# A two-layer trunk in fp32: compression by strided operands, full-width splits with moves by DMA, mixer outputs in the stream's tile

## The chip, the core and the metric

One of the eight cores of a Trainium2 chip runs the kernel. Its engines are TensorE (PE: matmuls and transposes; PEld is the loading of its stationary operand), VectorE (DVE), ScalarE (ACT), GpSimd (POOL) and SyncE (SP), which here issues the DMA transfers. Every engine runs its own instructions strictly in the order in which they stand. The metric is the device time of one execution in microseconds (us).

## What is computed

Two layers over 512 tokens of 1024 channels, all in float32. A layer projects the stream once, gives the columns to three token mixers, joins their outputs by one projection, normalises, and runs a feed-forward block:

```python
def reference(x, w_in, cmp_pos, cmp_w1, ...):
    for l in range(DEPTH):
        proj = h @ w_in[l]
        nq, nkv, ngate, gq, gk, gv, glr, gog, pu = jnp.split(proj, split_points, axis=-1)
        mixed = jnp.concatenate([nsa_mixer(nq, nkv, ngate, ...),     # 6 query heads, 2 kv heads
                                 gla_mixer(gq, gk, gv, glr, gog, ..., gla_norm_g[l]),
                                 pool_mixer(pu, pool_w[l], pool_scale[l])], axis=-1)
        h = layer_norm(DEEPNORM_ALPHA * h + mixed @ w_out[l], ...)
        ff = jnp.square(jax.nn.relu(h @ w_up[l])) @ w_down[l]
        h = layer_norm(DEEPNORM_ALPHA * h + ff, ...)

# in nsa_mixer: 31 blocks of 32 tokens, 16 apart, are compressed to one key and one value each
    def compress(t, p, w1, w2):
        tb = t[:, :, blk_idx] + p                 # blk_idx = 16 n + 0..31; p: position table
        hid = jax.nn.gelu(tb.reshape(B, G, n_cmp, CMP_BLOCK * Dh) @ w1)
        return hid @ w2
# its three branches (compressed, selected, window) are softmax attentions with one gate per head and branch;
# pool_mixer subtracts a token from trailing means over 2, 4, 8 and 16 tokens and maps each group
```

## The kernel before

A Python program writes the instructions out. Its `Planner` (line 33) keeps a planned time for every engine and buffer; each helper (`MM`, `TR`, `act`, `tt`, `ts`, `stt`, `recip`, `dma`) emits one instruction and adds its estimated cost. Pieces of work are generators with a priority: whenever the planned TensorE time `now` has reached what a piece waits for, its next step is emitted; when none is ready, the backbone `everything()` emits more matmuls of the projections. So the estimates set the order of instructions on every engine, and the chip then runs that order. Since all calls go through helpers, all matmuls have line 177, transposes 182, ACT work 190, tensor-tensor 202, tensor-scalar 208, `stt` 215, reductions 219, reciprocals 227, loads 318. `tt(..., "any")` lets the planner choose between DVE and POOL.

Every fp32 product is three TensorE passes over fp32r halves: an operand is split by ACT into a rounded high part (`wh`, `hTh`) and by DVE or POOL into the rest (`wl`, `hTl`). Weights come by DMA as `wr` into four raw buffers and are split into four pairs of `wh`/`wl`; `splits()` does it in the order of use.

The backbone of a layer runs the blocks of `ORDER = 'ABDEFWGCOPNR'`: A, B, E, D, F, G, C, O project the stream (A and O token-major, O being the gate `og` of the linear-attention mixer in 128x384 matmuls; G the queries; D the compressed branch's keys and values and one more key; F the third key; C the pooling mixer's input; E values and gates), W is the compression, P and R the two halves of the early output projection, N its remaining rows for the first tokens; the feed-forward block follows. Attention, linear attention and pooling run as pieces beside it.

What the change touches: `im2col` builds, from the keys and values of `k0_out`/`v0_out`, tiles of 4 x 124 shifted columns plus positions (64 partitions at a time, with a step of 16 tokens), splits them, and `compress` reads them as 32 contiguous pairs of matmuls of 248 and 124 columns per program; `hidden` adds the halves. `q_out` and `k_out` split 64 partitions at a time, so that a tile holds the high half in one set of 64 partitions and the low half in the other. `u_out` makes prefix sums for windows 2 to 16: a POOL copy of the first 1, 2, 4 or 8 columns and one addition each, then a 512-column matmul with `wbd`. `head` makes scores, reduces their maxima, exponentiates on ACT (the sum goes to `den`), clamps `den`, takes the reciprocal f, multiplies it by the head's gate, scales the exponentials `s` by it on whichever engine the planner thinks first, and transposes them (`ident`). `og_out` makes the swish gate and multiplies by `ngh`, half the norm's weights broadcast to 128 partitions. `gla_mix` and the end of `head` put split mixer outputs into slots (a common pool of `NSLOT` 128x512 tiles), which `mix_parts` hands to `out_part` and `out_rest`. `new_hT` makes the tiles hTh and hTl of the transposed stream.

## Time and profile before

| | |
|---|---|
| median of 3 runs | 1217.43 us (1216.94 to 1217.57) |
| the profiled execution | 1217.37 us |
| its span, first to last instruction | 1215.6 us |
| mean granted TensorE clock | 0.994 of full |
| TensorE busy | 98% |
| DVE, ACT, POOL busy | 75%, 49%, 25% |
| DMA, mean rate | 94 GB/s |

The span is cut into instructions of five engines. A busy TensorE is not TensorE at its peak: matmuls overlap, so the distance between the starts of two is what one costs. Idle time of another engine costs nothing by itself. What ended TensorE's idle time is named behind `<-`. Layer 0 takes roughly the first 600 us and the mixers' stage the first 200 us of each layer.

### The profile page before, as it was taken

What the parts mean: (1) busy time and instruction counts of PE and PEld (TensorE: products, weight loads), DVE (VectorE), ACT (ScalarE), POOL (GpSimd) and SP (SyncE); (2) the same over time, 40 slices, a digit from 0 to 9 for tenths busy, and PEclk for the clock granted to TensorE, in tenths of its full rate; (3) what the DMA queues carried; (4) which work ended last, traced back from release to release, by engine and by line L of the source; (5) the groups of instructions that cost most, each with busy time, mean ns of one, the idle gap of its engine ahead of it and who ended that gap; (6) DMA issues with size and microseconds to landing.
All of it is one profiled execution on the core that took longest, in us unless ns stands there. A gap on an engine that the chain in (4) does not pass through costs nothing.

```text
span 1215.6 us, 19049 instructions
## 1 busy us (share of the span) xinstructions
PE 1192.5 (98%) x7305; PEld 1050.1 (86%) x7305; DVE 909.3 (75%) x1563; ACT 593.2 (49%) x1119; POOL 308.5 (25%) x332
## 2 busy tenths in 40 slices
PE   9999999999999999999999998999999999999997
PEld 7898788889889899899888977888998998998985
DVE  3699998886687476485667999979947864855846
ACT  4633666554337246255146445766633562552730
POOL 0255431234330010020132634303434200201202
PEclk9999999999999999999999999999999999999999
DMA  6514103143323333335144040121623233342331
GB/s 215 149 40 118 44 19 103 30 138 121 88 71 121 103 88 121 87 87 153 41 134 115 27 131 18 55 77 36 183 71 94 87 122 87 88 125 82 98 112 69
DMA packets 128523, 113.92 MB, mean 94 GB/s; under 512 B 17168, under 2 KB 103728, under 8 KB 128432
## 3 DMA queue, kind: packets, MB, share of 16 engines
q1 hardware_dynamic: 128432, 112.71, 31.1%
q8 instruction: 57, 0.93, 0.3%
q14 instruction: 34, 0.28, 0.1%
HBM read 110.59 MB, written 2.10 MB: 93 GB/s over the span
## 4 chain that ended last, share of the span: by engine, by line
PE 84%; DVE 11%; POOL 2%; ACT 1%; issue 1%; DMA 1%; POOLq 0%; SPq 0%; DVEq 0%
PE b L177 81%; DVE s L202 4%; PE b L182 3%; DVE s L215 2%; DVE nb L219 1%; POOL r L202 1%; DVE wl L202 1%; ACT s L190 1%; POOL s L202 1%; DVE h L215 0%; DMA h<-in_x_dram 0%; DVE s L208 0%; DMA wr<-in_w_up_dram 0%; DVE den L208 0%; DVE f L227 0%
## 5 line engine op out<-in xcount | busy, mean ns | idle before, releaser
L177 PE MATMUL b<-wh,s 128*128 128x512 f32 x1280 | 413.9, 397 | 0.5 <-ACT s L190 0.5
L202 DVE TENSOR_TENSOR wl<-wr,wh 128x1024 fp32r<-128x1024 f32 (+4 forms) x185 | 226.6, 1228 | 163.1 <-ACT wh L190 155.0
L190 ACT ACTIVATE wh<-wr 128x1024 fp32r<-128x1024 f32 (+4 forms) x194 | 184.4, 954 | 252.2 <-PE b L177 205.3
L177 PEld LDWEIGHTS b<-wh,s 128*128 128x128 f32 x1280 | 240.5, 188 | 54.9 <-ACT s L190 0.9
L177 PE MATMUL b<-wl,s 128*128 128x512 f32 x640 | 252.4, 394 | 0.0
L190 ACT ACTIVATE s<-s 128x512 fp32r<-128x512 f32 (+5 forms) x328 | 186.9, 587 | 99.1 <-DVE s L202 79.3
L177 PE MATMUL b<-s,s 128*128 128x256 f32 (+5 forms) x1296 | 183.7, 293 | 0.2
L190 ACT ACTIVATE s<-b 128x384 fp32r<-128x384 f32 (+8 forms) x230 | 106.5, 475 | 156.2 <-PE b L177 116.8
L177 PE MATMUL b<-hTh,wh 128*128 128x256 f32 (+1 forms) x544 | 176.0, 324 | 0.0
L177 PE MATMUL b<-hTh,wl 128*128 128x256 f32 (+1 forms) x544 | 174.6, 321 | 0.0
L177 PE MATMUL b<-hTl,wh 128*128 128x256 f32 (+1 forms) x544 | 174.4, 321 | 0.0
L177 PEld LDWEIGHTS b<-s,s 128*128 128x128 f32 (+1 forms) x1296 | 163.2, 190 | 5.2 <-DVE s L202 1.4
L202 DVE TENSOR_TENSOR s<-s,s 128x512 fp32r<-128x512 f32 (+6 forms) x190 | 145.2, 774 | 21.6 <-ACT s L190 16.0
L202 DVE TENSOR_TENSOR s<-b,s 128x256 f32<-128x256 f32 (+7 forms) x262 | 123.9, 482 | 46.4 <-PE b L177 38.1
L177 PEld LDWEIGHTS b<-wl,s 128*128 128x128 f32 x640 | 120.4, 188 | 26.5 <-POOL wl L202 0.7
L202 POOL TENSOR_TENSOR s<-wr 128x512 f32<-128x512 f32 x24 | 39.1, 1631 | 319.8 <-DMA wr<-in_w_up_dram 288.3
L177 PEld LDWEIGHTS b<-hTh,wl 128*128 128x128 f32 x544 | 102.5, 188 | 8.6
L177 PE MATMUL b<-hTh,s 128*128 128x256 f32 x576 | 109.9, 284 | 0.0
L177 PEld LDWEIGHTS b<-hTh,wh 128*128 128x128 f32 x544 | 102.5, 189 | 8.2
L177 PEld LDWEIGHTS b<-hTl,wh 128*128 128x128 f32 x544 | 102.5, 188 | 8.0
L202 POOL TENSOR_TENSOR s<-s,s 128x512 f32<-128x512 f32 (+5 forms) x54 | 72.7, 1348 | 135.7 <-DVE s L202 73.5
L177 PEld LDWEIGHTS b<-hTh,s 128*128 128x128 f32 x576 | 92.1, 191 | 0.1
(150 smaller groups left out, 1618.4 us busy)
## 6 DMA issues: line engine op xcount, KB each, us to landing
wr<-in_w_down_dram SPq DMA_DIRECT2D x64, 512.0 KB, 3.8
wr<-in_w_up_dram SPq DMA_DIRECT2D x52, 512.0 KB, 4.0
wr<-in_w_out_dram SPq DMA_DIRECT2D x20, 512.0 KB, 3.5
wr<-in_w_in_dram SPq DMA_DIRECT2D x24, 384.0 KB, 3.2
...
wr<-in_w_in_dram SPq DMA_DIRECT2D x6, 512.0 KB, 3.7
h<-in_x_dram SPq DMA_DIRECT2D x4, 512.0 KB, 8.4
```

The costliest lines, as they stand in the source:

```text
L177: nc.tensor.matmul(o, a, b, start=start, stop=stop, **({"skip_group_check": True} if loose else {}))
L182: nc.tensor.transpose(o, a, i)
L190: nc.scalar.activation(o, a, func, scale=scale, **kw)
L202: e.tensor_tensor(out=o, in0=a, in1=b, op=op)
L215: nc.vector.scalar_tensor_tensor(o, a, s, b, op0=op0, op1=op1)
L219: nc.vector.tensor_reduce(o, a, axis=AX.X, op=op, negate=negate)
```

## The change

- Compression: `im2col` is gone. Keys and values are split into a tile X of 128 x 8 x 560 (`to_windows`); two DMAs of `move`, SBUF to SBUF on SP's queue, put the copy shifted by one token into the other 64 partitions. `positions` writes the position table into 32 further columns, as another block. `compress` reads X with a step of 16 elements, 2 x 2 x 2 x 34 = 272 columns and 136 for the low pass; `hidden` takes the positions' contribution from one column (`hb`) and adds it.
- A move is a plain `dma_start` with both sides bitcast to fp32; the planner counts 0.5 us on the queue and 2.0 to the landing.
- Queries and keys: one full-width ACT instruction and one DVE or POOL instruction per tile instead of halves, and three or six moves of 64x512.
- `u_out`: the copies of the first columns go from POOL to ACT.
- `head`: f is made by one DVE instruction, min with 1e30 and product with the gate, instead of clamp on DVE and product on POOL or DVE.
- `og_out`: no product with `ngh`; the w_out rows are scaled instead when they are split (`scaled`, with `gsc` of 128x3).
- Mixer outputs go into the slices of hT that the stream no longer needs, behind the event `gone` of block O; compressed probabilities and two of the feed-forward's token sums go into tiles with X's tag; `NSLOT` 46 becomes 38.
- The planner's estimate for an fp32r matmul is max(0.109, 0.006 + 0.4414e-3 n), 0.224 for fp32, 0.04 for bf16.

```diff
     def MM(o, a, b, start, stop, loose=False):
         n = b.free_size()
-        pl.pe(max(0.025, n / 2400.0 * (4 if b.dtype == F32 else 1) + 0.0025))
+        pl.pe(max(0.109, 0.006 + 0.4414e-3 * n) if b.dtype == F32R else 0.224 if b.dtype == F32 else 0.04)
         nc.tensor.matmul(o, a, b, start=start, stop=stop, **({"skip_group_check": True} if loose else {}))
...
-            yield from split_to(hi, lo, raws[i], firsts.get(i, -0.2))
+            if i in scaled:
+                l, ks = scaled[i]
+                yield [(l, "params"), free_act]
+                for j, k in enumerate(ks):
+                    if 3 <= k < 6:
+                        act(hi[:, j], raws[i][:, j], scale=gsc[l][:, k - 3:k - 2])
+                    else:
+                        act(hi[:, j], raws[i][:, j])
+                yield
+                for j, k in enumerate(ks):
+                    yield [free_dve]
+                    if 3 <= k < 6:
+                        stt(lo[:, j], raws[i][:, j], gsc[l][:, k - 3:k - 2], hi[:, j], OP.mult, OP.subtract)
+                    else:
+                        tt(lo[:, j], raws[i][:, j], hi[:, j], OP.subtract)
+            else:
+                yield from split_to(hi, lo, raws[i], firsts.get(i, -0.2))
...
-        ngh = layer.tile([128, 384], F32, tag="ngh", name=f"ngh{l}")
+        gsc[l] = layer.tile([128, 3], F32, tag="gsc", name=f"gsc{l}")
...
             free()
-            yield
-            tt(gd, gd, ngh, OP.mult, "any")
             yield [E("on", t)]
             tt(on[t], on[t], gd, OP.mult, "any")
...
-            mh, ml = slot(n=384, dt=F32R), slot(n=384, dt=F32R)
-            act(mh, p[:, 0:384])
-            yield
-            tt(ml, p[:, 0:384], mh, OP.subtract)
+            pv = p[:, 0:384].rearrange("p (k n) -> p k n", k=3)
+            mh, ml = [a[:, 0:3, 128 * t:128 * t + 128] for a in hT]
+            act(mh, pv)
+            yield
+            tt(ml, pv, mh, OP.subtract)
             free()
-            gmix[t] = (mh, ml)
...
-            if k < 3:
-                mt, c0 = nmix[t // 2][k], 128 * (t % 2)
-                return mt[:, c0:c0 + 128], mt[:, 256 + c0:384 + c0]
             if k < 6:
-                return [a[:, 128 * (k - 3):128 * (k - 3) + 128] for a in gmix[t]]
+                return [a[:, (k + 3) % 6, 128 * t:128 * t + 128] for a in hT]
             return [a[:, 128 * t:128 * t + 128] for a in mix[k]]
...
-                    ts(nw[r, 0:sh], prev[r, 0:sh], 1.0, None, OP.mult, eng="pool")
+                    act(nw[r, 0:sh], prev[r, 0:sh])
                     tt(nw[r, sh:512], prev[r, sh:512], prev[r, 0:512 - sh], OP.add, "any")
...
+        def own(X, kv, g, part):
+            return X[64 * g:64 * g + 64, 4 * part + 2 * kv + g, 1 - g:513 - g]
+        def other(X, kv, g):
+            return [X[64 * q:64 * q + 64, 2 * kv + g:8:4, 1 - q:513 - q] for q in (1 - g, g)]
+        def to_windows(kv, src, eng):
+            X = xs[0]
+            for g in range(2):
+                act(own(X, kv, g, 0), src[64 * g:64 * g + 64])
+            yield
+            for g in range(2):
+                tt(own(X, kv, g, 1), src[64 * g:64 * g + 64], own(X, kv, g, 0), OP.subtract, eng)
+            yield
+            for g in range(2):
+                move(*other(X, kv, g))
+            yield
...
         def k0_out(ps):
-            kv0[0] = yield from rope(ps)
-            ev("k0")
+            r = yield from rope(ps)
+            yield
+            yield from to_windows(0, r, "any")
+            drop()
+            ev("im", 0)
         def v0_out(ps):
-            kv0[1] = slot()
-            act(kv0[1], ps)
+            yield from to_windows(1, ps, "dve")
             free()
-            ev("v0")
-            yield
+            ev("im", 1)
         def k_out(br):
             def out_(ps):
                 r = yield from rope(ps)
                 yield
-                res = []
-                for g in range(2):
-                    kh, kl = slot(dt=F32R), slot(dt=F32R)
-                    src = r[64 * g:64 * g + 64]
-                    act(kh[0:64], src)
-                    act(kh[64:128], src)
-                    res.append((kh, kl))
-                    yield
-                    hs = kh[64 * g:64 * g + 64]
-                    tt(kl[0:64], src, hs, OP.subtract, "any")
-                    tt(kl[64:128], src, hs, OP.subtract, "any")
+                own_ = [slot(dt=F32R), slot(dt=F32R)]
+                act(own_[0], r)
+                yield
+                tt(own_[1], r, own_[0], OP.subtract, "any")
                 drop()
-                KK[br] = res
+                yield
+                both = [slot(dt=F32R), slot(dt=F32R)]
+                for a, b in zip(both, own_):
+                    move(a[0:64], b[64:128])
+                    move(a[64:128], b[64:128])
+                yield
+                for a in own_:
+                    move(a[64:128], a[0:64])
+                yield
+                KK[br] = [own_, both]
                 ev("K", br)
             return out_
...
             def out_(ps):
                 r = yield from rope(ps)
                 yield
-                for e in range(2):
-                    q_ = slot(dt=F32R)
-                    me, ot = slice(64 * e, 64 * e + 64), slice(64 - 64 * e, 128 - 64 * e)
-                    act(q_[me], r[me], scale=0.125)
-                    yield
-                    stt(q_[ot], r[me], 0.125, q_[me], OP.mult, OP.subtract)
-                    QS[2 * m + e] = q_
-                    ev("Q", 2 * m + e)
+                q0, lo = slot(dt=F32R), slot(dt=F32R)
+                act(q0, r, scale=0.125)
+                yield
+                stt(lo, r, 0.125, q0, OP.mult, OP.subtract)
                 drop()
+                yield
+                q1 = slot(dt=F32R)
+                move(q1[0:64], q0[64:128])
+                move(q1[64:128], lo[64:128])
+                yield
+                move(q0[64:128], lo[0:64])
+                yield
+                drop()
+                QS[2 * m], QS[2 * m + 1] = q0, q1
+                ev("Q", 2 * m)
+                ev("Q", 2 * m + 1)
             return out_
-        ims = [None] * 4
-        def im2col():
...
-                            sap = bass.AP(tensor=a.tensor, offset=a.offset + t0, ap=[a.ap[0], [2, 4], [16, 31]])
...
-                            tt(imv[64 * par:64 * par + 64, :, c0:c0 + 31], sap, pa[:, :, None].to_broadcast([64, 4, 31]),
-                               OP.add, "any")
...
-                ev("im", jc)
-            drop(2)
+        xs = [big.tile([128, 8, 560], F32R, tag="X", name=f"X{l}")]
+        def positions():
...
+                act(hi, pv)
+                yield
+                tt(lo, pv, hi, OP.subtract)
+            yield
+            ev("im", 2)
         def compress():
             yield [("bank", 1)]
             ph = bank()
-            for jc in range(4):
-                yield [E("im", jc), ("split", u["W"][jc // 2])]
-                wh, wl = parts[u["W"][jc // 2]]
-                for j in range(4):
-                    kk = 4 * (jc % 2) + j
-                    hl = ims[jc][j // 2][:, j % 2]
-                    MM(ph[:, 0:248], wh[:, kk, :], hl, jc == 0 and j == 0, False, True)
-                    MM(ph[:, 0:124], wl[:, kk, :], hl[:, 0], False, jc == 3 and j == 3, True)
...
+            X = xs[0]
+            yield [E("im", i) for i in range(3)]
+            for j in range(16):
+                ui = u["W"][j // 8]
+                yield [("split", ui)]
+                wh, wl = parts[ui]
+                c0 = 1 + 2 * j
+                MM(ph[:, 0:272], wh[:, j % 8, :], X[:, :, c0:c0 + 529:16], j == 0, False, True)
+                MM(ph[:, 0:136], wl[:, j % 8, :], X[:, 0:4, c0:c0 + 529:16], False, j == 15, True)
+                if j % 8 == 7:
+                    used(ui)
...
+            hb = small(1, "hb", bufs=2)
+            hxv = hx.rearrange("p (g n) -> p g n", g=2)
+            phv = ph[:, 0:272].rearrange("p (a k g n) -> p a k g n", a=2, k=2, g=2)
+            for kv in range(2):
+                r = slice(64 * kv, 64 * kv + 64)
+                vcopy(hxv[r], phv[r, 1, kv, :, 0:31])
+                vcopy(hb[r], phv[r, 1, kv, 0, 32:33])
+                tt(hb[r], phv[r, 0, kv, 0, 32:33], hb[r], OP.add)
+                stt(hxv[r], phv[r, 0, kv, :, 0:31], hb[r], hxv[r], OP.add, OP.add)
...
-            res = slot(dt=F32R), slot(dt=F32R)
+            res = room(2 * H), room(2 * H + 1)
...
-            ts(den, den, 1e-30, None, OP.max)
             recip(f, den)
-            yield
-            tt(f, f, gate[:, 2 * H:2 * H + 2, 3 * hh + br], OP.mult, "any")
+            stt(f, f, 1e30, gate[:, 2 * H:2 * H + 2, 3 * hh + br], OP.min, OP.mult)
...
-                mt = slot(dt=F32R)
-                act(mt[:, 0:256], f_)
-                yield
-                tt(mt[:, 256:512], f_, mt[:, 0:256], OP.subtract)
+                yield [E("gone", 2 * H), E("gone", 2 * H + 1)]
+                mh, ml = [a[:, 3 + m, 256 * H:256 * H + 256] for a in hT]
+                act(mh, f_)
+                yield
+                tt(ml, f_, mh, OP.subtract)
                 drop()
-                nmix[H][m] = mt
                 ev("nmix", H, m)
...
+                if name == "O":
+                    ev("gone", t)
...
-NSLOT = 46
+NSLOT = 38
```

How the order of instructions changes at three places of layer 0. The first is TensorE's order around the pool mixer's first matmul (`wbd`). In the rows of before, `b_1443` is a 128-token tile of block O, whose weight split `wl_1451` is read there, and s_1387 and s_1421 are scaled exponentials; in the rows of after, `s_855`, `s_856` are a key's high and low parts, `s_1258` is a query and `b_1370` the first head's scores. Before:

```order
L177 MATMUL b_1443<-wh_1308,hTh_117 128x384
L177 MATMUL b_1443<-wl_1309,hTh_117 128x384
L177 MATMUL b_1443<-wh_1308,hTl_118 128x384
L177 MATMUL b_1535<-s_1452,wbd_128 128x512
L182 MATMUL b_1548<-ident,s_1387 128x128 x3
L182 MATMUL b_1556<-ident,s_1421 128x128 x3
L177 MATMUL b_1443<-wh_1450,hTh_117 128x384
L177 MATMUL b_1443<-wl_1451,hTh_117 128x384
L177 MATMUL b_1443<-wh_1450,hTl_118 128x384
```

After:

```order
L177 MATMUL b_1322<-wl_1274,hTh 128x384
L177 MATMUL b_1322<-wh_1273,hTl 128x384
L177 MATMUL b_1370<-s_855,s_1258 128x128
L177 MATMUL b_1370<-s_856,s_1258 128x128
L177 LDWEIGHTS identb
L177 MATMUL b_1370<-mdiag,identb 128x128
L177 MATMUL b_1370<-s_855,s_1258 128x256
L177 MATMUL b_1370<-s_856,s_1258 128x256
L177 LDWEIGHTS identb
L177 MATMUL b_1370<-mdiag,identb 128x128
L177 MATMUL b_1377<-s_1340,wbd_128 128x512
```

The six transposes of exponentials have left the place behind the pool mixer's matmul; a head's scores stand ahead of it now.

The second is POOL's order in the same stretch: before, the last of the prefix sums (`s_1478` to `s_1487`), the products f with the gate, the scaling of a head's exponentials, and a weight split of block O:

```order
L202 TENSOR_TENSOR s_1478<-s_1441 128x511
L208 TENSOR_SCALAR s_1481<-s_1478 128x2
L202 TENSOR_TENSOR s_1481<-s_1478 128x510
L208 TENSOR_SCALAR s_1484<-s_1481 128x4
L208 TENSOR_SCALAR s_1487<-s_1484 64x8
L202 TENSOR_TENSOR f_1327<-f_1327,gate_131 128x2
L202 TENSOR_TENSOR f_1338<-f_1338,gate_131 128x2
L202 TENSOR_TENSOR s_1421<-s_1421,f_1338 128x128
L202 TENSOR_TENSOR s_1421<-s_1421,f_1338 128x256
L202 TENSOR_TENSOR wl_1451<-wr_1224,wh_1450 128x768
```

After, from the first prefix addition of C's output to the linear mixer's products behind the split of the same unit of block O:

```order
L202 TENSOR_TENSOR s_1317<-s_1314 64x510
L202 TENSOR_TENSOR s_1348<-s_1320 128x511
L202 TENSOR_TENSOR s_1354<-s_1351 128x508
L202 TENSOR_TENSOR wl_1330<-wr_1185,wh_1329 128x768
L202 TENSOR_TENSOR s_1450<-s_1450,f_1369 128x256
L202 TENSOR_TENSOR s_798<-s_798,s_1489 128x384
L202 TENSOR_TENSOR s_816<-s_816,s_1557 128x384
```

The copies of the first columns and the two products f with the gate have left POOL's queue ahead of the split of block O's last unit; some of the additions have gone to DVE.

The third is SP's order from block O's last unit on, where `wr` are weight loads. Before:

```order
L318 DMA wr_1224<-in_w_in_dram 128x2x384
L318 DMA wr_1253<-in_w_out_dram 128x2x512
L318 DMA wr_1306<-in_w_out_dram 128x2x512
L318 DMA wr_1357<-in_w_out_dram 128x512
L318 DMA wr_1572<-in_w_out_dram 128x1024
L318 DMA wr_2017<-in_w_out_dram 128x1024
```

After, with `s_1258`, `s_1261`, `s_1278` the high parts of the three query tiles and `s_1259`, `s_1262`, `s_1279` the low parts:

```order
L322 DMA wr_1185<-in_w_in_dram 128x2x384
L322 DMA wr_1214<-in_w_out_dram 128x2x512
L322 DMA wr_1271<-in_w_out_dram 128x2x512
L328 DMA s_1288<-s_1258 64x512
L328 DMA s_1288<-s_1259 64x512
L328 DMA s_1291<-s_1261 64x512
L328 DMA s_1291<-s_1262 64x512
L322 DMA wr_1301<-in_w_out_dram 128x512
L328 DMA s_1311<-s_1278 64x512
L328 DMA s_1311<-s_1279 64x512
L328 DMA s_1258<-s_1259 64x512
L328 DMA s_1261<-s_1262 64x512
```

Moves of 64x512 have come between the loads of the output projection's weights, and one load stands among them.

## Rows read from the trace of the kernel before

**Rows 1.** Page, busy time, share and instructions of each engine.
```profile
PE 1192.5 (98%) x7305; PEld 1050.1 (86%) x7305; DVE 909.3 (75%) x1563; ACT 593.2 (49%) x1119; POOL 308.5 (25%) x332
```

**Rows 2.** Groups of PE: busy us, mean ns | idle us before, by releaser.
```profile
L177 PE MATMUL b<-wh,hTh 128*128 128x400 f32 (+2 forms) x192 | 66.8, 348 | 1.9 <-DVE s L215 1.7 <-ACT hTh L190 0.2
L177 PE MATMUL b<-wl,hTh 128*128 128x400 f32 (+2 forms) x192 | 64.2, 334 | 4.1 <-POOL wl L202 2.3 <-DVE wl L202 1.8
L182 PE MATMUL b<-ident,s 128*128 128x128 f32 (+2 forms) x294 | 45.5, 275 | 3.6 <-ACT s L190 2.1 <-DVE s L208 1.1 <-DVE s L202 0.3
...
L177 PE MATMUL b<-s,wh 128*128 128x256 f32 (+1 forms) x224 | 42.6, 288 | 1.1 <-POOL s L202 1.1
...
L177 PE MATMUL b<-s,wbd 128*128 128x512 f32 x8 | 4.2, 611 | 0.6 <-DVE s L202 0.6
```

**Rows 3.** Timeline of PE, gate block, layer 0: start us, us, instruction, [idle before].
```profile
137.79 0.34 PE L177 MATMUL b<-wl,hTh 128*128 128x384 f32 x1
137.97 0.34 PE L177 MATMUL b<-wh,hTl 128*128 128x384 f32 x1
...
140.73 1.20 PE L182 MATMUL b<-ident,s 128*128 128x128 f32 x6 [1.03 <-ACT s L190]
...
143.26 0.69 PE L177 MATMUL b<-wl,hTh 128*128 128x384 f32 x1 [1.16 <-POOL wl L202]
```

**Rows 4.** Timeline of DVE, POOL and ACT, the same stretch: a head's factor f.
```profile
133.91 0.17 DVE L227 RECIPROCAL f<-den 128x2 f32<-128x2 f32 x1
...
139.25 0.71 POOL L208 TENSOR_SCALAR s<-s 64x8 f32<-64x8 f32 x1 [1.67 <-DVE s L202]
...
140.04 0.35 POOL L202 TENSOR_TENSOR f<-f,gate 128x2 f32<-128x2 f32 x2
...
140.27 0.40 ACT L190 ACTIVATE s<-s,f 128x128 f32<-128x128 f32 x1 [4.47 <-POOL f L202]
```

**Rows 5.** Windows: stretch, us, each engine's busy us, PEclk, DMA share, GB/s.
```profile
122.00:152.00 30.00, 27.45 (x156) 23.23 (x155) 28.64 (x70) 18.23 (x51) 12.76 (x23) 0.94 0.14 45
152.00:182.00 30.00, 28.29 (x206) 25.92 (x206) 29.12 (x84) 20.23 (x62) 10.74 (x20) 1.00 0.06 19
143.00:146.50 3.50, 3.24 (x11) 3.24 (x12) 3.26 (x13) 2.20 (x7) 1.41 (x4) 0.56 0.45 150
743.00:746.50 3.50, 3.17 (x10) 3.17 (x11) 3.26 (x13) 2.21 (x7) 1.47 (x4) 0.56 0.47 150
```

**Rows 6.** Timeline of PE at the compression of layer 0 and the block behind.
```profile
98.73 0.33 PE L177 MATMUL b<-s,wh 128*128 128x248 f32 x1
...
98.96 0.33 PE L177 MATMUL b<-s,wh 128*128 128x248 f32 x1
...
99.95 0.38 PE L177 MATMUL b<-s,wh 128*128 128x248 f32 x1 [0.60 <-POOL s L202]
...
100.74 0.39 PE L177 MATMUL b<-hTl,wh 128*128 128x512 f32 x1
100.97 0.39 PE L177 MATMUL b<-hTh,wl 128*128 128x512 f32 x1
```

**Rows 7.** Groups of DVE by form, 60 to 280 us.
```profile
L208 DVE TENSOR_SCALAR den<-den 128x2 f32<-128x2 f32 x24 | 5.9, 247 | 0.1
...
L208 DVE TENSOR_SCALAR s<-s,f 128x384 f32<-128x384 f32 x6 | 2.5, 411 | 0.3 <-POOL f L202 0.3
```

**Rows 8.** Tile posT: ns of one (min/median/max), first and last start, forms.
```profile
L202 DVE TENSOR_TENSOR s<-s,posT x40: 345/363/1281, 72.7 to 693.0; 64x124 f32<-64x124 f32 x40
```

**Rows 9.** Timeline of DVE: a contiguous half-height product, and layer 0's first query shuffle.
```profile
114.38 0.28 DVE L202 TENSOR_TENSOR s<-b,cf 64x128 f32<-64x128 f32 x1
...
116.03 0.73 DVE L916 STREAM_SHUFFLE s<-b 128x512 f32<-128x512 f32 x1
```

**Rows 10.** Page, DMA issues: count, KB each, median us to landing.
```profile
wr<-in_w_down_dram SPq DMA_DIRECT2D x64, 512.0 KB, 3.8
...
w<-in_cmp_w_dram SPq DMA_DIRECT2D x6, 16.0 KB, 2.2
```

81 lines of the change are left out of this document (38 added, 43 removed).

## The prediction

> **What bounds the kernel now.** I read the page's busy shares first: TensorE is busy for 98% of the span, no other engine above 75% [rows 1]. What a change can give is therefore only what TensorE's line loses between matmuls, or what its matmuls cost more or less. Next I read the groups of TensorE's instructions for the last column, the idle time and what ended it [rows 2]: 1.1 us before the block compression's matmuls (ended by POOL), 0.6 before the pool mixer's (DVE), 2.1 + 1.1 + 0.3 before the heads' transposes (ACT, DVE, DVE) and 2.3 before the token-major gate block (POOL), where 1.7 more wait for DVE's line L215: 9.2 us, in two layers, all in the mixers' stage. The 1.8 us behind DVE's wl is at the layer boundary, which no edit reaches. TensorE's timeline shows two of them in their place [rows 3]: it waits 1.03 us for ACT at 140.7, and 1.16 us for a weight split on POOL at 143.3.
>
> Why is ACT late there? The timelines of DVE, POOL and ACT, read backwards [rows 4]: ACT stood 4.47 us until POOL had made f, the product of a head's 1/den and its gate. DVE had finished the reciprocal at 134.08, but POOL began the product only at 140.04. It runs in order, and ahead of the product stood a copy of 64x8 from the pool mixer's prefix sums, which itself waited 1.67 us for DVE. The weight split that TensorE misses at 143.3 stands behind the product on POOL. So a few tiny POOL instructions make both waits.
>
> The windows give the rest [rows 5]. [...] Each layer has this once: 2 x 3.5 x (1 - 0.56) = 3.1 us. The same view shows the limit of any gain: DVE is busy 28.64 and 29.12 of 30 us there.
>
> A wait costs slightly more than its idle time: around the compress wait the starts are 99.95 - 98.96 = 0.99 apart where the pair before took 0.23, with 0.60 waited [rows 6], so 0.16 per wait on top.
>
> **The change part by part.**
>
> *f on DVE, prefix copies on ACT.* POOL loses the products of f and the copies; the order shows that what is left before the gate block's split are three prefix additions. f becomes one more DVE instruction of the reciprocal's size, 0.17 us [rows 4], directly behind it, and the clamp of den leaves DVE: 24 per layer at 0.247 = 5.9 us off [rows 7], 24 x 0.17 = 4.1 on. Scaling of the exponentials moves from ACT to DVE for 12 tiles per layer; 128x384 costs 0.411 [rows 7], smaller ones less, so about 4.4 us on. The query splits become 3 full-width instead of 6 half-height instructions of the same 512 columns: about 2 us off. DVE's sum after the queries stays where it is (-5.9 + 4.1 + 4.4 - 2). This takes away the waits for ACT (2.1) and for POOL's wl (2.3), and with them the clock's fall (3.1). The pool mixer's matmul now stands behind a head's scores, so its wait goes (0.6), and I count the single 0.3.
>
> *Compression.* im2col goes: 64 additions of 64x124 per program, 40 of them on DVE at 0.363 [rows 8], with their copies and splits. Instead each of the two inputs (keys, values) gets two copies on ACT, two subtractions of 64x512 and two moves. From the end of block D to the first compress matmul stand two other blocks, E and F: 24 matmuls of 512 columns at 0.23 [rows 6] = 5.5 us, and 96 of 274. The new chain is a shuffle and three more DVE steps, two splits and one move (2.2 to 3.8 us, below), some 10 us. E's 96, at 0.127 each in proportion to the 0.18 of 384 columns [rows 3], take 12 us more, so the wait of 1.1 goes.
>
> Its matmuls get wider (272 and 136 columns for 248 and 124; 32 pairs) and their moving operand is read with a step of 64 bytes. The trace has no matmul that reads like this. At the contiguous rate, 36 more columns at 0.23/512 = 0.45 ns are 0.016 us per pair, +0.5 us in all. The nearest row for the step is DVE's position addition, which reads with the same 64 bytes: 0.363 us for 64x124, against 0.28 for a contiguous 64x128 [rows 9]; that ratio of 1.3 on a pair of 0.25 gives 0.32, +2.9 us. I take the middle, 0.28 per pair: **+1.7 us**. It is all on TensorE's path.
>
> [...]
>
> *Full-width splits and moves.* A move is a DMA from SBUF to SBUF of 128 KB (64 rows of 2 KB) or 256 KB. The trace has none; loads of 16 KB land after 2.2 us and loads of 512 KB after 3.8 [rows 10]. I take 2.4, near the small one, and keep 3.8 as the upper end. Queries need two in series, as the second overwrites what the first reads. From the first query shuffle to the first low half the order has 11 DVE instructions, at about the shuffle's 0.73 [rows 9] 8 us; if the shuffle starts with the end of block G, queries 0 and 1 are ready 8 + 4.8 = 12.8 us behind G. The first head stands behind all of block C and 18 matmuls of the gate block: 48 x 0.23 [rows 6] + 18 x 0.18 [rows 3] = 14.3. So the moves are hidden, with 1.5 us to spare; at 3.8 each they are 1.3 late. SP runs in order too: the weight load among the query moves waits for a free buffer, and moves behind it wait with it.
>
> *Mixer outputs in hT, TX and probabilities in new tiles, scaled w_out units, gsc for ngh.* The same arithmetic in other places. The outputs must wait until the gate block has read hT, but they are only needed by the output projection behind the last heads; the multiplication by ngh leaves og's chain. I count nothing. If that cover fails, it is one more wait like that at L215, 1.7 / 2 = 0.85 us per layer.
>
> *TensorE's estimates.* They only set the order. The matmuls are the same 7175, apart from the 32 pairs.
>
> **The sum.** Gone: 1.1 + 0.6 + 2.1 + 2.3 + 0.3 = 6.4 us of waiting, nine waits x 0.16 = 1.4 on top, 3.1 of clock: 10.9. Added: 1.7 for the strided read. What DVE ends today (1.7 + 1.1 = 2.8) stays; because its load in the stage does not fall and the waits that hid DVE's work go away, I let it come twice: +2.8. The profiled execution took 1217.37 us, 1.8 more than its span and practically the median (1217.43): 1217.4 - 10.9 + 1.7 + 2.8 = **1211.0**.
>
> **The rivals.** About 0.2% (2.4 us) is what a measurement of this kernel can tell from no change.
>
> *The strided operand is slow (slower).* Place: the 32 pairs of compression. Per element DVE's strided row costs, above the fixed part of some 0.15 us, (0.363 - 0.15)/124 = 1.72 ns; if TensorE reads at that rate, 408 columns take 0.70 us per pair, and (0.70 - 0.23) x 32 = +15 us instead of 1.7: 1211.0 + 13.3 = 1224. It decides against the kernel by more than 0.2% from (1219.8 - 1209.3) / 32 + 0.23 = 0.56 per pair. For it: the same step, and 272 different places per partition. Against: DVE and TensorE need not read in the same way. If it is true at half (0.47 per pair) the result is near 1217. [...]
>
> *DVE is the bound of the stage.* Removing POOL's lateness only lets TensorE reach DVE's lateness earlier: DVE has 1.36 and 0.88 us free in 30 [rows 5]. Then only compression's wait goes (1.1 + 0.3), the clock falls as before, and the strided read costs 1.7: 1217.7, or up to 1220 with one more wait of 1 us per layer. For it: nearly full windows, and f and the scaling moving towards DVE. Against: the 6 us between reciprocal and product were not DVE's; its load before the queries falls by some 7 us per layer.
>
> *Moves late.* At 3.8 us each, or queued behind a weight load, the first heads start 1.3 to 4 us late per layer, and the clock may fall in the gap: 1211 + 2.6 to 1211 + 8 = 1213.6 to 1219.
>
> *Everything goes.* The 2.8 us of DVE's waits and their 0.6 go too, and the step costs nothing: 1217.4 - 10.9 - 3.4 + 0.5 = 1203.6.
>
> **How the numbers follow.** Chances: the forecast, 1205 to 1214.9, 0.53; everything goes 0.10; both faster by over 0.2%, 0.63. DVE as the bound 0.17 (0.12 within 0.2%, 0.05 slower). Moves late 0.08 (0.05 within, 0.03 slower). Strided operand slow 0.12, slower. So same 0.17, slower 0.20. The range runs from just under "everything goes", 1203, to 1221, which takes in DVE as the bound and late moves and leaves out the strided operand at its full price.
>
> **What the profile after would show.** Right: no f on POOL, ACT's scaling within 1 us of the reciprocal; no wait above 0.5 us before the six transposes and the gate block; full granted clock in the second half of the stage in both layers; compress starting without a wait and its pairs 0.25 to 0.32 apart; the first scores without a wait for a DMA. Wrong: pairs above 0.5 apart; a wait of scores ended by a DMA from s to s; a new group before transposes or output matmuls that DVE ends, above 5.6 us in all; or a clock of 0.5 that has only moved to another place.

## The result and the profile after

The changed kernel takes 1228.42 us (median of 4 runs, 1227.29 to 1229.49), the kernel before 1217.5 beside it (1216.94 to 1219.11): a ratio of 1.0087 [1.007, 1.0105], so 10.6 us slower. The forecast was 1211, and its range ended at 1221. The profiled execution took 1229.01 us with a span of 1227.0, 11.4 more than the span before.

The page of after, busy time of each engine, against [rows 1]:

```profile
PE 1196.8 (98%) x7305; PEld 1053.5 (86%) x7305; DVE 891.2 (73%) x1575; ACT 574.9 (47%) x1091; POOL 221.6 (18%) x208
```

DVE, ACT and POOL each lost work (18, 18 and 87 us), as the diff says. TensorE, which has 82% of the chain that ended last, gained 4.3. So the work that left the other engines bought nothing, and the question is what TensorE waits for. Its groups in after (busy us, mean ns | idle us before, by what ended it), against [rows 2]:

```profile
L177 PE MATMUL b<-hTh,wl 128*128 128x256 f32 (+1 forms) x544 | 175.2, 322 | 1.8 <-DVE wl L202 1.8
...
L177 PE MATMUL b<-s,s 128*128 128x256 f32 (+4 forms) x1008 | 149.2, 299 | 4.8 <-DVE s L202 2.6 <-DMA s<-s 2.1
...
L177 PE MATMUL b<-wl,hTh 128*128 128x512 f32 (+3 forms) x288 | 100.4, 349 | 0.9 <-DVE wl L202 0.5 <-POOL wl L202 0.4
...
L177 PE MATMUL b<-hTl,s 128*128 128x256 f32 x288 | 81.7, 284 | 3.5 <-DVE hTl L202 3.5
L182 PE MATMUL b<-ident,s 128*128 128x128 f32 (+2 forms) x294 | 46.7, 284 | 8.4 <-ACT s L190 3.6 <-DVE s L208 2.7 <-DMA s<-in_cmp_pos_dram 1.5
```

The waits that I wanted gone are gone: of POOL's 2.3 before the gate block's 128x384 matmuls nothing is left (the 0.4 above stands at 620.65 us, before a 128x400 matmul), and the compression's 1.1 and the pool mixer's 0.6 have no successor (`X,wh` and `s,wbd` wait 0.0). But others stand in their place. By the two pages, span less busy time, TensorE is idle for 30.2 us, and was for 23.1: +7.1. The groups above hold 19.4 of it; of the transposes' 8.4, 1.5 belong to two transposes of the position table that wait for its load, early in each layer. Four of the waits in their place, in order of time, and between them two neighbouring pairs of the compression (start us, us, instruction, [idle before]):

```profile
33.01 0.50 PE L177 MATMUL b<-hTh,wl 128*128 128x512 f32 x1 [1.78 <-DVE wl L202]
...
99.24 0.42 PE L177 MATMUL b<-X,wh 128*128 128x272 f32 x1
...
99.60 0.42 PE L177 MATMUL b<-X,wh 128*128 128x272 f32 x1
...
137.57 0.41 PE L177 MATMUL b<-s,s 128*128 128x128 f32 x2 [0.94 <-DMA s<-s]
...
174.97 0.78 PE L182 MATMUL b<-ident,s 128*128 128x128 f32 x3 [1.34 <-ACT s L190]
...
261.10 0.38 PE L177 MATMUL b<-hTl,s 128*128 128x256 f32 x1 [1.73 <-DVE hTl L202]
```

The pairs are 0.36 apart, where [rows 6] has 0.23: 32 x 0.13 = +4.2 us, and TensorE's busy time grew by 4.3. With the +7.1 of idle time that is 11.3 of the 11.4 us between the spans. The wait at 174.97 ends with ACT again, and again through f, but behind DVE this time. DVE and ACT there:

```profile
172.56 1.15 DVE L219 TENSOR_REDUCE nb<-b 128x1 f32<-128x128 f32 x4
...
174.09 0.14 DVE L227 RECIPROCAL f<-den 128x2 f32<-128x2 f32 x1
...
174.52 0.40 ACT L190 ACTIVATE s<-s,f 128x128 f32<-128x128 f32 x1 [2.63 <-DVE f L215]
```

No POOL instruction stands between reciprocal and scaling now. ACT still waits 2.63 us, since the reciprocal itself comes late: DVE works through the maxima of other heads first. Behind this wait the clock falls as it did before; windows (stretch, us, busy us of each engine, granted clock, DMA share, GB/s), against [rows 5]:

```profile
122.00:152.00 30.00, 28.56 (x160) 24.79 (x159) 27.64 (x59) 12.11 (x36) 9.19 (x7) 1.00 0.32 94
152.00:182.00 30.00, 26.03 (x182) 23.41 (x180) 28.57 (x97) 18.99 (x65) 7.88 (x13) 0.94 0.01 2
178.00:181.00 3.00, 3.00 (x14) 2.28 (x13) 2.75 (x12) 2.88 (x13) 0.62 (x1) 0.52 0.02 5
782.00:786.00 4.00, 3.40 (x15) 2.58 (x15) 3.74 (x14) 2.73 (x12) 0.62 (x1) 0.62 0.00 0
```

The first half of the stage has the full clock; the fall now stands in the second, once per layer: 3 x (1 - 0.52) + 4 x (1 - 0.62) = 3.0 us, as much as the 3.1 before. DVE is nearly as full as it was.

### The profile page after: what moved, and what is told of

It reads as the page before. It is cut to its first block, busy times and chain, and to the rows that moved or that the text cites. A ratio compares the mean times of both kernels' runs of the same rounds, so it can differ in the third digit from the quotient of the medians.

```text
span 1227.0 us, 18953 instructions
## 1 busy us (share of the span) xinstructions
PE 1196.8 (98%) x7305; PEld 1053.5 (86%) x7305; DVE 891.2 (73%) x1575; ACT 574.9 (47%) x1091; POOL 221.6 (18%) x208
## 4 chain that ended last, share of the span: by engine, by line
PE 82%; DVE 11%; SPq 2%; DMA 2%; issue 1%; ACT 1%; POOL 0%; POOLq 0%; DVEq 0%; ACTq 0%
PE b L177 81%; DVE s L202 3%; SPq L322 2%; PE b L182 2%; DVE nb L219 2%; DVE h L215 1%; DVE hTl L202 1%; DVE s L208 1%; DVE s L215 1%; DVE f L215 1%; DMA wr<-in_w_in_dram 1%; ACT s L190 1%; DVE wl L202 0%; DMA h<-in_x_dram 0%; POOL s L202 0%
## 5 line engine op out<-in xcount | busy, mean ns | idle before, releaser
L177 PE MATMUL b<-wh,s 128*128 128x512 f32 x1088 | 347.6, 395 | 0.0
L177 PEld LDWEIGHTS b<-wh,s 128*128 128x128 f32 x1088 | 204.3, 188 | 47.3
L177 PE MATMUL b<-wl,s 128*128 128x512 f32 x544 | 214.5, 394 | 0.0
L190 ACT ACTIVATE s<-s 128x512 fp32r<-128x512 f32 (+6 forms) x286 | 164.2, 585 | 95.4 <-DVE s L202 88.6
L190 ACT ACTIVATE s<-b 128x256 f32<-128x256 f32 (+8 forms) x212 | 98.3, 476 | 125.1 <-PE b L177 105.9
L177 PE MATMUL b<-s,s 128*128 128x256 f32 (+4 forms) x1008 | 149.2, 299 | 4.8 <-DVE s L202 2.6
L177 PEld LDWEIGHTS b<-s,s 128*128 128x128 f32 (+1 forms) x1008 | 127.5, 192 | 11.3 <-issue 4.7
L202 DVE TENSOR_TENSOR s<-s,s 128x512 fp32r<-128x512 f32 (+2 forms) x164 | 118.5, 732 | 17.6 <-ACT s L190 13.2
L177 PEld LDWEIGHTS b<-hTh,wl 128*128 128x128 f32 x544 | 103.0, 189 | 10.9 <-DVE wl L202 2.2
L177 PE MATMUL b<-wh,hTh 128*128 128x512 f32 (+3 forms) x288 | 105.9, 368 | 0.0
L177 PE MATMUL b<-wl,hTh 128*128 128x512 f32 (+3 forms) x288 | 100.4, 349 | 0.9 <-DVE wl L202 0.5
L177 PE MATMUL b<-wh,hTl 128*128 128x512 f32 (+3 forms) x288 | 100.1, 348 | 0.0
```

The lines of the kernel that those rows point to most:

```text
L177: nc.tensor.matmul(o, a, b, start=start, stop=stop, **({"skip_group_check": True} if loose else {}))
L190: nc.scalar.activation(o, a, func, scale=scale, **kw)
L202: e.tensor_tensor(out=o, in0=a, in1=b, op=op)
```

## The experiments

The question is whether the edits cost the time, or the order that they make the planner write. With the order goes the choice of engine, where a piece may run on more than one: the planner makes both from its estimates, and no run here separates them. In the runs named "held" the planner still books the old instruction on the old engine, so that the order of every other instruction stays word for word that of the kernel that was edited; only the edited instruction differs (`planned_any`, `planned_move` and `pl.op` book, and do nothing else).

**One part taken out of after.** The compression reads neighbouring columns instead of every sixteenth (its compressed keys and values are then not the right ones):

```diff
-MM(ph[:, 0:272], wh[:, j % 8, :], X[:, :, c0:c0 + 529:16], j == 0, False, True)
-MM(ph[:, 0:136], wl[:, j % 8, :], X[:, 0:4, c0:c0 + 529:16], False, j == 15, True)
+MM(ph[:, 0:272], wh[:, j % 8, :], X[:, :, c0:c0 + 34], j == 0, False, True)
+MM(ph[:, 0:136], wl[:, j % 8, :], X[:, 0:4, c0:c0 + 34], False, j == 15, True)
```

> The changed kernel with the compression's 64 matmuls reading 34 neighbouring columns per row of X instead of columns 16 apart: same shapes, same instructions in the same order, other data (the compressed keys and values are wrong). Theory S (the strided read itself costs TensorE time): a pair of 272 and 136 columns, 0.36 us apart in the changed kernel's trace, goes to about 0.25; 32 x 0.11 = 3.5 us less, 1228.4 - 3.5 = 1224.9. Rival (the wider matmul costs 0.36 whatever the step): pairs stay at 0.36, 1228.4 within 1.5.

1225.57 us, 1.0074 [1.0052, 1.0095]. Two neighbouring pairs of this kernel:

```profile
97.54 0.34 PE L177 MATMUL b<-X,wh 128*128 128x272 f32 x1
...
97.79 0.34 PE L177 MATMUL b<-X,wh 128*128 128x272 f32 x1
```

They are 0.25 apart, and in the median of all pairs 0.24, with the same columns; after's median is 0.36. So the 64-byte step costs 0.12 x 32 = 3.8 us in the trace. In the time the difference to after is 2.9 us, and the two intervals overlap.

The wait of 1.78 us at 33.0 stands behind three mask casts on DVE. They go to GpSimd, the order held:

```diff
-vcopy(mdiag, cb[:, 0:128])
...
+    nc.gpsimd.tensor_copy(o_, a_)
+    pl.op("dve", 0.065 + 0.52e-3 * o_.free_size(), [o_], [a_])
```

> The changed kernel with the three casts of the masks (they wait for a load that lands at 31.5 us) on GpSimd instead of DVE, all other orders held, so that the three weight splits behind them on DVE no longer wait. Theory C: the wait of 1.8 us for a weight split at 33 us of layer 0 goes; 1.5 to 2 us less, 1226 to 1227. Rival: another wait takes its place, no change.

1226.32, 1.0085 [1.0067, 1.0104]: the wait is gone, a new one of 0.6 us, for ACT, stands before the transposes of `glr`, and against the kernel before the time doesn't show it. Both edits together:

> The changed kernel with both held edits at once: contiguous compression operand (wrong data) and the casts on GpSimd. If the two costs add, 1228.4 - 2.9 - 2.1 = 1223.4, and some 6 us above the kernel before are left to the order and the waits it brought. If one hid the other, 1225.5 or more.

1224.3, 1.0054 [1.0038, 1.0071]: some 4 us less than after. 6.6 remain (0.0054 of the time), for the other edits and for the order with its waits.

Queries and keys split in halves, without moves (the functions `q_out` and `k_out` as they stand in the kernel before, the `-` lines of the change; the order free):

> The changed kernel with the query and key splits of the kernel before (64 partitions at a time, no moves there); the moves of the compression stay. Theory M (the moves bring the first head about 11 us later, the gate block is used up while TensorE waits for them, and the heads at the end have nothing beside them): the first scores stand before the end of block C again, no wait for a DMA, the waits of 1.5 + 1.5 us before transposes late in the stage shrink; 5 to 10 us less, 1218 to 1223. Rival E (the new TensorE estimates make the order that loses the time): 1228.4 within 2.4, since the estimates stay.

1243.02, 1.0222 [1.0206, 1.0237]: slower by 14.6 than with the moves. The same for queries alone with the order held:

```diff
-act(q0, r, scale=0.125)
+act(q0[0:64], r[0:64], scale=0.125)
+nc.scalar.activation(q1_[64:128], r[64:128], AF.Copy, scale=0.125)
...
-move(q1[0:64], q0[64:128])
+planned_move(q1, q0)
```

> The changed kernel with the query splits done on 64 partitions at a time as before and no query moves, the planner still counting full-width splits and moves, so that all orders stay (18 DMAs fewer, 6 more ACT and 6 more DVE instructions of half the height). Theory M2 (the wait for the moves costs what TensorE's line shows there, 0.9 us and refill per layer, and no more): the wait ended by a DMA goes, 1 to 3 us less, 1225.5 to 1227.5. Rival (the moves also hold up SP's weight loads or share memory with others): 5 us less or more. If the moves were hidden: no change within 1.5.

1235.1, 1.0143 [1.0128, 1.0158]. The scores no longer wait for a DMA, but in its groups DVE has taken its place, and more:

```profile
L177 PE MATMUL b<-s,s 128*128 128x256 f32 (+4 forms) x1008 | 149.9, 300 | 5.2 <-DVE s L202 3.9 <-DVE s L215 1.0
...
L177 PE MATMUL b<-s,wbd 128*128 128x512 f32 x8 | 5.8, 813 | 1.6 <-DVE s L202 1.6
```

So the moves are late by 2.1 us, and in this order those of the queries are still worth 6.7: their lateness isn't what makes the kernel slow. The keys' moves weren't taken out with the order held. The planner's old estimate of a matmul, with all other edits:

```diff
-pl.pe(max(0.109, 0.006 + 0.4414e-3 * n) if b.dtype == F32R else 0.224 if b.dtype == F32 else 0.04)
+pl.pe(max(0.025, n / 2400.0 * (4 if b.dtype == F32 else 1) + 0.0025))
```

> The changed kernel with the planner's TensorE estimates of the kernel before. Theory E: the waits of 1.8 us at 33 us (a weight split behind three casts), of 1.7 us before matmuls with hTl at 261 us, and of 1.3 + 1.3 us before transposes at 174 to 177 us were made by the new estimates and go; 6 to 10 us less, 1218 to 1222. Theory M: only those away from the heads go (1.8 once, 1.7 twice), the heads still start late; 1222 to 1226. If the estimates were a gain, 1230 or more.

1241.43, 1.02 [1.0185, 1.0215]: 13 us slower than after, though the old estimates are those with which the kernel before runs in 1217.

**One part put into before.** The new estimates alone, without any edit of the work (the diff just above the other way round):

> The kernel before with only the changed kernel's TensorE estimates: same instructions, another order. In the changed kernel going back to the old estimates cost 13 us. Theory O (the order, not the edits, carries most of the difference, and its effect has no fixed sign): outside 1217 plus or minus 3, on either side. Rival (better estimates make a better order): 1205 to 1213.

1241.21, 1.0202 [1.0186, 1.0218]: +24.8 us, from an estimate. (By its page DVE has 44 instructions more than in before, POOL 38 and ACT 6 fewer.) The parts do not add: the new estimates alone cost 24.8, all other edits alone 24.6, and both together, as the change, some 11. And the smallest change of this kind that I could make, the transposes' estimate, by 4 ns:

```diff
-pl.pe(0.056)
+pl.pe(0.060)
```

> The kernel before with the planner's estimate of one transpose raised from 0.056 to 0.060 us, and nothing else: the same instructions, except that the planner may choose another engine here and there, in an order that moves some 1170 of 7292 TensorE instructions. Theory O (any new order of this stage costs much, whatever caused it): 1222 or more. Rival (only estimates that are wrong by much make a bad order): 1217 plus or minus 2.4.

1227.5, 1.0082 [1.0064, 1.01]. As many microseconds as the whole change, and the work is the same: by the expectation's count some 1170 of 7292 TensorE instructions stand in another place, and a few pieces run on another engine (by the page DVE has 12 instructions more, POOL 8 and ACT 4 fewer). A group of before, and two of this kernel:

```profile
L182 PE MATMUL b<-ident,h 128*128 128x128 f32 x128 | 19.3, 278 | 1.7 <-DMA h<-in_x_dram 1.3 <-DVE h L215 0.4
...
L182 PE MATMUL b<-ident,h 128*128 128x128 f32 x128 | 19.5, 280 | 6.7 <-DVE h L215 5.2 <-DMA h<-in_x_dram 1.5
...
L182 PE MATMUL b<-ident,s 128*128 128x128 f32 (+2 forms) x294 | 45.3, 277 | 6.6 <-DVE s L202 4.4 <-ACT s L190 2.1
```

The transposes of the stream, at another stage, wait 5.2 us for DVE where they waited 0.4. Next f on DVE and the prefix copies on ACT, the order free:

```diff
-ts(nw[r, 0:sh], prev[r, 0:sh], 1.0, None, OP.mult, eng="pool")
+act(nw[r, 0:sh], prev[r, 0:sh])
...
-ts(den, den, 1e-30, None, OP.max)
 recip(f, den)
-yield
-tt(f, f, gate[:, 2 * H:2 * H + 2, 3 * hh + br], OP.mult, "any")
+stt(f, f, 1e30, gate[:, 2 * H:2 * H + 2, 3 * hh + br], OP.min, OP.mult)
```

> The kernel before with only two edits: a head's f made by one DVE instruction behind the reciprocal, and the prefix sums' copies on ACT. The prediction's step (POOL's lateness makes the two waits of 1.03 and 1.16 us per layer and the fall of the clock): these go and 5 to 9 us with them, 1208.5 to 1212.5. Rival (DVE is the bound of the stage): the waits come back behind DVE, the clock falls elsewhere, 1217.5 within 2.4.

1235.33, 1.0158 [1.0141, 1.0175]. ACT in this kernel:

```profile
141.58 0.21 ACT L190 ACTIVATE s<-s 64x8 f32<-64x8 f32 x1 [0.91 <-POOL s L202]
...
142.67 0.40 ACT L190 ACTIVATE s<-s,f 128x128 f32<-128x128 f32 x1 [0.89 <-DVE f L215]
```

The copies wait for POOL's additions, now on ACT, ahead of the scaling; TensorE's transposes wait 10.1 us, 9.9 of them for ACT. With the order held the same edits cost little. f in the place where POOL had its product, the clamp only booked:

```diff
-ts(den, den, 1e-30, None, OP.max)
+pl.op("dve", 0.065 + 0.52e-3 * 2, [den], [den])
 recip(f, den)
 yield
-tt(f, f, gate[:, 2 * H:2 * H + 2, 3 * hh + br], OP.mult, "any")
+nc.vector.scalar_tensor_tensor(f, f, 1e30, gt_, op0=OP.min, op1=OP.mult)
+planned_any(2, [f], [f, gt_])
```

> The kernel before with f made on DVE and den's clamp gone, the planner still counting a clamp and a POOL product, so that TensorE's, ACT's and SP's orders are word for word those of before, and POOL's too without the 48 products. Theory H (the prediction's step is right when the order is held: POOL's lateness makes the waits of 1.03 and 1.16 us per layer and the clock's fall): ACT's 4.47 us behind f go, the two waits per layer and the clock's fall of 3.1 us go, 5 to 9 us less, 1208 to 1212. Rival D (DVE takes over as the late engine): within 2.4 of 1217, with waits that DVE ends.

the copies alone on ACT:

```diff
-ts(nw[r, 0:sh], prev[r, 0:sh], 1.0, None, OP.mult, eng="pool")
+nc.scalar.activation(nw[r, 0:sh], prev[r, 0:sh], AF.Copy, scale=1.0)
+pl.op("pool", 0.09 + 1.0e-3 * sh, [nw], [prev])
```

> The kernel before with only the prefix sums' copies moved from POOL to ACT, the planner counting them on POOL: every other order is word for word that of before. Theory Q (a copy that waits for an addition holds up whatever stands behind it, on ACT as on POOL; ahead of the product f on POOL stand the additions now, of which the last needs a copy of ACT): POOL's product f comes earlier than 140.0 us, but ACT's exponentials stand behind the copies; -2 to +2 us, 1215 to 1219. If POOL's copies alone were the cause of the two waits, 5 to 9 us less.

both:

> Both edits at once on the kernel before, orders held as in the two others. The kernel with the same two edits and the planner free took 1235.3. Theory H: 1208 to 1213, so that 22 us or more of difference are the planner's new order alone. Rival: the two edits themselves cost the time (ACT held up by copies, DVE by products), 1225 or more, order held or not.

1221.4 (1.0036 [1.0023, 1.0049]), 1217.44 (1.0002 [0.9992, 1.0011]) and 1220.28 (1.0027 [1.0018, 1.0037]). Why the first is 4 us slower, in DVE's and ACT's timelines of f held:

```profile
132.96 0.23 DVE L234 RECIPROCAL f<-den 128x2 f32<-128x2 f32 x2
...
142.26 0.23 DVE L1181 SCALAR_TENSOR_TENSOR f<-f,gate 128x2 f32<-128x2 f32 x2
...
142.50 0.80 ACT L190 ACTIVATE s<-s,f 128x128 f32<-128x128 f32 x2 [7.44 <-DVE f L1181]
```

The product stands 9 us of DVE's queue behind its reciprocal, so ACT waits longer than it did for POOL [rows 4]. Put directly behind the reciprocal, the planner's booking left where it was:

```diff
 recip(f, den)
+nc.vector.scalar_tensor_tensor(f, f, 1e30, gt_, op0=OP.min, op1=OP.mult)
 yield
-tt(f, f, gate[:, 2 * H:2 * H + 2, 3 * hh + br], OP.mult, "any")
+planned_any(2, [f], [f, gt_])
```

> As b_fheld (the kernel before, f on DVE without den's clamp, all other orders held), but the product stands directly behind its reciprocal on DVE instead of where the planner had put POOL's product, 9 us of DVE work later. Theory P (the place in the queue decides, not the engine): ACT's scaling follows the reciprocal at 133 us within 1 us, the waits of 1.03 and 1.16 us per layer go or shrink below 0.4, and the clock stays; 3 to 8 us less than before, 1209 to 1214. Rival (the step is wrong: DVE is the bound of the stage): 1217 or more.

and with the copies on ACT:

> As b_fnear, with the prefix sums' copies on ACT as well (order held). b_cpheld took 1217.4, so the copies alone did nothing. Theory P: within 2 us of b_fnear, 1209 to 1214. If ACT, held up by copies that wait for additions, delays the exponentials and scalings: 2 to 6 us above b_fnear.

1215.96 (0.9998 [0.9988, 1.0007]) and 1217.41 (1.0008 [0.9999, 1.0018]). The second has both edits that my forecast rested on, f and the copies, in the order of before; the first has f alone. Neither gains anything that can be measured. The first one's window, its groups on TensorE, ACT's scaling, and the pool mixer's second pair of matmuls with the DVE addition ahead of it:

```profile
122.00:152.00 30.00, 26.75 (x166) 22.68 (x164) 28.64 (x73) 18.76 (x52) 11.74 (x18) 1.00 0.13 45
...
L177 PE MATMUL b<-wl,hTh 128*128 128x400 f32 (+2 forms) x192 | 62.5, 325 | 4.1 <-POOL wl L202 2.3 <-DVE wl L202 1.8
...
L182 PE MATMUL b<-ident,s 128*128 128x128 f32 (+2 forms) x294 | 45.7, 275 | 3.6 <-DVE s L202 2.4 <-DVE s L215 1.1
...
L177 PE MATMUL b<-s,wbd 128*128 128x512 f32 x8 | 4.4, 630 | 2.7 <-issue 2.1 <-DVE s L202 0.6
...
134.23 0.80 ACT L190 ACTIVATE s<-s,f 128x128 f32<-128x128 f32 x2
...
145.73 0.17 DVE L202 TENSOR_TENSOR s<-t,s 64x16 f32<-64x16 f32 x1
...
146.00 1.10 PE L177 MATMUL b<-s,wbd 128*128 128x512 f32 x2 [1.05 <-issue]
```

ACT scales at 134.23 without a wait, and the clock is full in this execution (1.00 for 0.94). But the granted clock differs between executions of one kernel: its mean was 0.994 to 0.998 in the ten of this kernel, and 0.994 to 0.998 in the eighteen of before beside them, so a full clock in one profile need not be a gain of the edit. TensorE's transposes wait 3.6 us as they did, for DVE instead of ACT. POOL's split is as late as before without its product, since the copy of 64x8 that waits for DVE still stands ahead of it. And the pool mixer's matmuls wait 2.7 instead of 0.6; for 2.1 of it the profile names no releaser ("issue"), but DVE's addition ends at 145.90, just ahead of the start at 146.00. In the second kernel, with the copies off POOL too:

```profile
L177 PE MATMUL b<-wl,hTh 128*128 128x400 f32 (+2 forms) x192 | 64.2, 334 | 1.8 <-DVE wl L202 1.8
...
L182 PE MATMUL b<-ident,s 128*128 128x128 f32 (+2 forms) x294 | 46.7, 282 | 2.1 <-DVE s L215 1.1 <-ACT s L190 0.9
...
L177 PE MATMUL b<-s,wbd 128*128 128x512 f32 x8 | 5.2, 734 | 5.1 <-DVE s L202 5.1
```

POOL's 2.3 us are gone and ACT's 2.1 are 0.9, and the pool mixer's matmuls wait 5.1 for DVE: what one wait gives, the next takes.

**POOL against DVE.** Can the rest be had? All three kernels have f near its reciprocal and the order held. First each prefix copy on the engine of its addition:

```diff
+e_ = nc.gpsimd if on_pool - on_dve < 0.1 else nc.vector
+e_.tensor_scalar(nw[r, 0:sh], prev[r, 0:sh], 1.0, None, op0=OP.mult)
```

> As b_fnear (the kernel before, f on DVE directly behind its reciprocal, orders held), with each prefix copy on the engine that makes the addition of the same step, so that no copy waits for another engine ahead of a weight split. In b_fnear the copy of 64x8 on POOL still waited 1.67 us for DVE, and the weight split behind it kept TensorE waiting 1.16 us per layer. Theory P: that wait goes in both layers, the clock stays at full, and part of it comes back at DVE: 1211 to 1214.5. Rival D (what one wait gives the next one takes, since DVE works 28 to 29 of 30 us there): within 2.4 of 1216.4.

Then, on top, the gate block's weight splits on DVE at POOL's place in the order (`phys` is the engine that does the work, while the planner books its own), and POOL's scaling on ACT:

```diff
-tt(lo, r, hi, OP.subtract, "any", bias)
+tt(lo, r, hi, OP.subtract, "any", bias, phys)
...
-tt(Ps[i], Ps[i], f[:, i:i + 1].to_broadcast([128, n]), OP.mult, "pool")
+nc.scalar.activation(Ps[i], Ps[i], AF.Copy, scale=f[:, i:i + 1])
```

> As b_best, with only the weight split of block O on DVE and the scaling of exponentials on ACT instead of GpSimd. Theory G: DVE's chain to the pool mixer's matmul, held up by that split for 1.5 us in b_best, runs through; the wait of 2.29 us before that matmul falls to about 1.3; 1 to 3 us less, 1213.5 to 1215.5. Rival D: within 2.4 of 1217.

And the other tensor-tensors of POOL in the stage on DVE too, the prefix additions first:

```diff
-tt(nw[r, sh:512], prev[r, sh:512], prev[r, 0:512 - sh], OP.add, "any")
+tt(nw[r, sh:512], prev[r, sh:512], prev[r, 0:512 - sh], OP.add, "any", phys="dve")
```

> As b_best (orders held, f directly behind its reciprocal), and in the heads' stage nearly all of GpSimd's work goes to others in the place where it stood: prefix additions and copies, gate products and the weight split of block O to DVE, scaling of exponentials to ACT. In the trace of before DVE instructions between 122 and 152 us that run beside a GpSimd tensor-tensor take 5.4 us longer in all than the same forms alone, and their ends fall on the GpSimd instruction's end. Theory G (GpSimd's tensor-tensors hold DVE up, so that work given to GpSimd is paid on DVE again): the small products of 64x16 fall from 1.0 to 1.7 us to 0.17, and DVE, though it does more, is not later; 2 to 6 us less than b_best's 1216.4, 1210.5 to 1214.5. [...]

1216.38 (0.9995 [0.9985, 1.0004]), 1222.91 (1.0046 [1.0028, 1.0064]) and 1226.65 (1.0074 [1.0058, 1.0091]). In the first, DVE's small additions and what POOL does beside them:

```profile
134.87 1.00 DVE L202 TENSOR_TENSOR s<-t,s 64x16 f32<-64x16 f32 x1
...
137.16 1.80 POOL L202 TENSOR_TENSOR wl<-wr,wh 128x768 fp32r<-128x768 f32 x1
137.27 1.72 DVE L202 TENSOR_TENSOR s<-t,s 64x16 f32<-64x16 f32 x1
139.25 1.49 PE L177 MATMUL b<-s,wbd 128*128 128x512 f32 x2 [2.29 <-DVE s L202]
```

DVE's addition of 64x16 runs for 1.72 us and ends at 138.99, POOL's split at 138.96; the pool mixer's matmul waits for it. In the third kernel nothing of POOL runs beside it, and the same addition and the displaced split read:

```profile
135.94 0.17 DVE L202 TENSOR_TENSOR s<-t,s 64x16 f32<-64x16 f32 x1
...
145.22 0.96 DVE L202 TENSOR_TENSOR wl<-wr,wh 128x768 fp32r<-128x768 f32 x1
...
146.24 0.69 PE L177 MATMUL b<-wl,hTh 128*128 128x384 f32 x1 [5.34 <-DVE wl L202]
```

0.17 us, for 1.72 beside POOL's split. But the split on DVE comes late in its queue, and TensorE waits 5.34. So in the last kernel, built on the second, the split stands where its inputs are ready:

```diff
 act(hi, r)
+if phys:
+    nc.vector.tensor_tensor(out=lo, in0=r, in1=hi, op=OP.subtract)
```

> As b_port2, with block O's weight split (now on DVE) emitted directly behind the high part on ACT: on DVE it stands ahead of the last two prefix additions and the maxima instead of 24 instructions later. In b_port2 TensorE waited 5.34 us per layer for that split, and the clock fell. Theory P (places in the queues, not the engines' load, make these waits): those 10.7 us go, some 1.5 us come back before the pool mixer's matmul, and the heads' stage gives 2 to 5 us against the kernel before: 1211 to 1215. Rival D (DVE's load bounds the stage, so TensorE waits for DVE a few us later): 1216 to 1219.

1215.03, 0.999 [0.9978, 1.0001]. The wait is gone; DVE's on the transposes is 4.4 us per program, and DVE is busy for 27.91 of the 30 us of 122 to 152. It is the fastest kernel that I ran, and not shown to be faster than before.

## Why the prediction was wrong

*TensorE's estimates.* "They only set the order" and counted nothing: this is the step that failed. The order is what the time hangs on here. One estimate, 4 ns higher, costs 10 us; the new ones alone 24.8; the old ones under the new edits 13; f and the copies cost 18 with the order free, and nothing that can be measured held and near (1.0008 [0.9999, 1.0018]). All six orders that the planner wrote anew, after's among them, took 10 to 26 us more than that of before. So the order of before is better than any of them, and an edit that makes the planner write another one pays for it; why it is so good, no run shows. The sum had no term for this: by it the waits were to fall by 5.0 (6.4 + 1.4 - 2.8), and they rose by 7.1; the clock was to give back 3.1 and gave 0.1; the strided read took 4.2 for 1.7. These three make 17.6 us, and the forecast missed by 17.4. That the 7.1 of waits belong to after's order as a whole and not to one edit is my reading of these runs, and not shown: what all edits of the change would take in the order of before wasn't tried, since compression and moves have no place there. (The "same 7175" stands in no row: TensorE has 7305 instructions before [rows 1] and after.)

*Gone, 10.9.* Right in what it named, wrong in what it was worth. With both edits and the order held, POOL's wait went and ACT's shrank as told, and the time stayed at 1217.41. I let DVE's 2.8 come twice; in that run the pool mixer's matmuls alone wait 5.1 for it. The clock's 3.1 I had read from one execution, 3.5 us at 0.56 in each layer [rows 5], and that it goes with the waits was my estimate, which no run shows: with f alone near its reciprocal TensorE still waited 1.16 us for POOL's split, at 141.38, and the clock was 1.00 from 122 to 152. The rival "DVE is the bound of the stage" named this mechanism: without compression's part and the strided read it says 1217.4, and the runs with f near its reciprocal took 1215.96 and 1217.41. After didn't come out there, as it also has another order. Two of the signs that I had named for being wrong came: scores that wait for a DMA from s to s, and a clock near 0.5 that has only moved.

*Strided operand.* The sign was right and the size too small: 0.36 per pair, 3.8 us for the step and 4.2 with the width, for 1.7. My upper end from DVE's row was 0.32. With the order and the columns the same, 408 per pair, the traces show 0.36 us at a step of 64 bytes and 0.24 with neighbouring columns. By the rate of the rival "the strided operand is slow" it would have been 0.70: it fell.

*Moves.* They land after longer than I took; after's page, DMA issues (count, KB each, median us to landing):

```profile
X<-X SPq DMA_DIRECT2D x8, 256.0 KB, 3.7
s<-s SPq DMA_DIRECT2D x42, 128.0 KB, 4.1
```

4.1 for 2.4, above my end of 3.8, and the first heads wait for it, 0.94 and 1.20 us, as the rival "moves late" said (1.3 per layer at 3.8). SP's order has a part in it too. The first query's high half on ACT, and SP's queue, in after:

```profile
125.71 0.63 ACT L190 ACTIVATE s<-s 128x512 fp32r<-128x512 f32 x1 [2.67 <-DVE s L202]
...
119.89 8.76 SPq L322 DMA_DIRECT2D wr<-in_w_out_dram  x2
128.75 2.39 SPq L328 DMA_DIRECT2D s<-s  x4
```

The half is ready at 126.34, but the second weight load ahead of the moves waits 7.9 us for its buffer, until DVE's split of `wr` ends at 128.25, so the first move starts at 128.75, 2.4 us later; without that load the wait of 0.94 might not be there (not run). That the full-width splits are worth it was right for the queries (6.7 us, order held).

*Mixer outputs in hT.* "I count nothing" can't be judged apart, as no run undoes it alone. The 3.5 us behind DVE's hTl are new, but they stand before the feed-forward's first matmuls (261.10 and 864.95), and what these wait for is the split of the newly transposed stream (`hTl<-b,hTh`, 128x512, on DVE from 260.37) and not a mixer output.

*Compression without a wait, no f on POOL.* As told, at 0.0 each.
